# A hybrid RG-LRU and RWKV-7 block: the inverse's products in the second recurrence issued unit by unit, its values loaded two steps ahead, its outputs stored with half the transfers

## The chip, the core and the metric

One program runs on one core of a Trainium2 chip. The metric is the device time of one execution in microseconds (us); lower is better. The core has TensorE (PE; its weight loads are listed as PEld), VectorE (DVE), ScalarE (ACT), GpSimd (POOL), and SyncE (SP), whose queue issues all the transfers of this kernel. Matrix products leave TensorE into PSUM, and DVE or ACT copy them to SBUF.

## The reference, cut to what matters

The block takes 1024 latent tokens of width 1024 and 256 context tokens. Two token mixers run on the same normalised input: a gated linear recurrence (the first recurrence), and RWKV-7 (the second), of 16 heads, in two directions. Their outputs are gated, projected, summed into the stream, and followed by a SwiGLU layer and a final norm. The change lies in RWKV-7's scan over a state `S` of 64x64 for each head and direction, whose output of both directions is then summed, normalised per head and gated:

```
def wkv7_scan(r, w, k, v, a, b, S0):
    def step(S, inp):
        r_t, w_t, k_t, v_t, a_t, b_t = inp
        sa = jnp.einsum('dbhij,dbhj->dbhi', S, a_t)
        S = S * w_t[..., None, :] + sa[..., :, None] * b_t[..., None, :] + v_t[..., :, None] * k_t[..., None, :]
        y = jnp.einsum('dbhij,dbhj->dbhi', S, r_t)
        return S, y
...
ys, S = wkv7_scan(orient(two(rr)), orient(heads(decay)), orient(kd), orient(two(vv)),
                  orient(two(-kk)), orient(kk[None] * heads(a)), S0)
```

All is float32.

## The kernel before

The program has stages. `phase0_h`, `phase_ux` and `phase_a2` make the normalised input, its projections, the first recurrence (`lru_tiles`, in 11 tiles of 120 channels), and the operands of the second one. `phase_b` runs the second recurrence. `phase_c1` and `phase_c2` do the output projections and the SwiGLU layer. The framework schedules: it places each instruction in the in-order queue of its engine by priority (mostly the order of the program text) and by when it reckons the operands ready, so the end of `phase_a2` and the start of `phase_b` run together.

**The second recurrence in blocks.** The scan is taken 32 tokens at a time: 1280 tokens make `NSTEP` = 40 steps, steps 0 to 7 over the context, 8 to 39 over the latents (these give outputs). A unit is one head in one direction, 32 in all. `wkv_chain(k, a)` drives one half, 8 heads in both directions, so 16 units; the two halves `a` = 0 and 1 are generators that `phase_b` (L1134) advances in a fixed pattern, so that one half's products stand between a product and the copy it waits for in the other half. Within a half step, in this order:

- **ru**: 16 products of a unit's 128 rows by 32 columns, tile `skb` times `tvu`, into the first half of a PSUM tile `t` (`ru`). Four neighbours go to four column groups of TensorE. A copy then moves the result to `rs`.
- **X**: the inverse of a unit's 32x32 triangular system, times `rs`, into the second half of the same PSUM tile. The 32x32 inverses were made in `phase_a2` (`wkv_inverse`, on DVE), stored to DRAM (`x_d`, `xc_d`) and come back as `xc`, four steps a tile. Before the change a block-diagonal 128x128 matrix `xbd` is built from `xc` for each four units, by four DVE copies of 32 partitions a step (L1025, both halves at once; two buffers `xbd0`, `xbd1`, with zeros off the diagonal), and the half step needs 4 products of 128x128 (L1046). A switch `UT` in the text, off here, holds the other way: 16 products of 32x32 straight from `xc`.
- four copies of 32 partitions put the result into `tvu[96:128]`.
- **pn**: 16 products, the next state, into `pn`; two copies (at every second step a multiplication by the decay `pb`, L1063) move it to rows 0 to 63 of the next step's `tvu`.
- **py**: for latent steps 16 products give the output; a copy to `ys`, then four stores of 32 partitions to `y_d`, rows of 256 numbers each (L1013).

One f32 product shows as two matmuls in the trace. The copies of `wkv_chain` go to DVE and ACT in a fixed rota, two of five to DVE (L993).

**Values.** Rows 64 to 95 of `tvu` are the step's values, loaded from `v_d` by `new_tvu` one step ahead into one of two buffers for each half (L969).

**What runs beside it.** `lru_out` (PE group `pol`, L1107, with loads `lh`, `lu`, `olr`, `olg` and work on ACT, POOL and DVE) is a filler: 480 products of 128x128 by 512, dealt out after the products X of each half. `wkv_load` brings `ska`, `skb` and `xc` up to three steps ahead. From step 28 on `norms` runs `group_norm` for blocks of 128 tokens as both directions finish them; it loads `y_d` back in one transfer for each direction (L1246). The last two blocks follow in `phase_c1`.

**The queue of SP.** It is in order, and a transfer waits in it for its operands, for its buffer, and for an earlier transfer to land: the program gives each transfer one of eight semaphores in turn.

Of the kernel before, what the change touches and what calls it, by code (L numbers as in the profile page):

```python
# [16 lines left out]
P = 128  # L17
D = 1024
# [891 lines left out]
FPTS = ((0, 0), (38, 1), (40, 1))  # L910
UT = 0
NEND = 3
SETV = 0
SETDVE = 0
XDVE = 40
XACT = 0
PACE = 1
# [12 lines left out]
def wkv_setup(k):  # L930
# [4 lines left out]
    for i, t in enumerate(k.ska):  # L935
        nc.scalar.copy(t[0:64], bcast(k.ident[0:64, 0:64], 1, NU))
    if not UT:
        k.xbd = [z(f"xbd{i}", [P, 8, 4, 32]) for i in range(2)]
        for t in k.xbd:
            (nc.vector if SETDVE & 2 else nc.gpsimd).memset(t, 0.0)  # L940
    k.tvu = [[z(f"tvu{a}_{i}", [P, 2, 8, 64]) for i in range(2)] for a in range(2)]
    k.pb = z("pb", [P, 2, 20, KD])
# [22 lines left out]
def new_tvu(k, s, a):  # L965
    nc = k.nc
    src = pair(k.v_d.rearrange("(c s) f -> c s f", s=32), chunk_id(s, 0), chunk_id(s, 1))
    t = k.tvu[a][s % 2]
    nc.sync.dma_start(t[64:96].rearrange("p d h i -> p d (h i)"), src[:, :, a * 512:a * 512 + 512].rearrange("d s f -> s d f"))  # L969
    return t  # L970
# [14 lines left out]
def wkv_chain(k, a):  # L985
# [13 lines left out]
    def outputs(s, tvu):  # L999
        if s < 8:  # L1000
            return
        skb = k.skb[s % NRING]
        py = k.psb2.tile([P, 4, 64], F32, name=f"py{s}_{a}", tag="py", bufs=1)
        for v, g, gr, d, i in units:
            mm(py[gr, v], skb[:, unit(d, i), 0:32], tvu[:, d, i])
        ys = k.op.tile([P, 256], F32, name=f"ys{s}_{a}", tag="ys", bufs=4)
        copy(ys, py.rearrange("p v i -> p (v i)"))
        for d in range(2):
            r = 32 * chunk_id(s, d)
            for h in range(2):  # L1010
                g = 2 * d + h
                c = a * 512 + h * 256
                nc.sync.dma_start(k.y_d[d, r:r + 32, c:c + 256], ys[32 * g:32 * g + 32])  # L1013

    cur, nxt, prev = None, new_tvu(k, 0, a), None
    for t in k.tvu[a]:
        (nc.vector if a < SETV else nc.gpsimd).memset(t[96:P], 0.0)
    for s in range(NSTEP):
        ska, skb = k.ska[s % NRING], k.skb[s % NRING]
        if not UT:  # L1020
            xb = k.xbd[s % 2]
        if a == 0 and not UT:
            for g in range(4):
                gr = slice(32 * g, 32 * g + 32)
                (nc.scalar.copy if s < XACT else nc.vector.tensor_copy if s < XDVE else nc.gpsimd.tensor_copy)(xb[gr, :, g], k.xc[s // 4][gr, s % 4].rearrange("p a v t -> p (a v) t"))  # L1025
        prev, tvu = cur, nxt
        cur = tvu
        ahead = lambda: new_tvu(k, s + 1, a) if s + 1 < NSTEP else None
        if a == 1:
            nxt = ahead()  # L1030
        t = ps.tile([P, 2, 4, 64], F32, name=f"ru{s}_{a}", tag="ru", bufs=2)
# [6 lines left out]
        if a == 0:  # L1038
            if s > 0:
                outputs(s - 1, prev)  # L1040
            nxt = ahead()
            yield
        for v, g, gr, d, i in units if UT else ():
            mm(t[gr, 1, v], k.xc[s // 4][gr, s % 4, a, v], r[gr, v])
        for v in range(0 if UT else 4):
            mm(t[:, 1, v], xb[:, a * 4 + v].rearrange("p a b -> p (a b)"), r[:, v])  # L1046
        for g in range(4):
# [186 lines left out]
def group_norm(k, pool, ps, tb, out=None):  # L1234
# [9 lines left out]
    y1 = k.c1p.tile([P, NH, 64], F32, name="gy1_7") if tb == 7 else big("gy1")  # L1244
    for t, src in ((v, k.v_d), (g, k.gate_d), (y, k.y_d[0]), (y1, k.y_d[1])):
        nc.sync.dma_start(flat(t), src[tok])  # L1246
        for _ in range(GNY):
            yield
# [252 lines left out]
def scratch(k):  # L1501
# [15 lines left out]
    k.t1_d = t("t1_d", [D, SEQ])  # L1517
    k.y_d = t("y_d", [2, SEQ, D])

# [176 lines left out]
```

## Time and profile before

| | |
|---|---|
| median of 3 runs | 3172.0 us (3169.22 to 3175.68) |
| the profiled execution | 3170.86 us, of which the profile spans 3168.8 us |
| PE busy | 2772.7 us (87%), 20606 matmuls |
| DVE busy | 2010.8 us (63%) |
| ACT busy | 1410.4 us (45%) |
| POOL busy | 1037.3 us (33%) |

The profile is one execution. Busy time of PE is the union of its matmuls; a matmul's duration holds its way through the array, so neighbours overlap, and the pace of a group is read from the starts. "PEclk" is the granted share of TensorE's clock: 1.0 is 2.4 GHz, 0.5 is 1.2 GHz, a value between them a mixture over time. "Idle before" is an engine's idle time just ahead of a group, with what ended it.

### The profile page before, as it was taken

The numbers are of one execution on the slowest core, as the hardware profiler recorded it, in microseconds if no ns is written. First come the engines' busy times: TensorE is split into PE (matmuls) and PEld (weight loads), VectorE is DVE, ScalarE is ACT, GpSimd is POOL, SyncE is SP. The second block draws the span as 40 slices with busy tenths as digits, with TensorE's granted clock in tenths as the row PEclk, the third lists the DMA queues.
The fourth block names the chain that finished last, engine by engine and source line by source line (L and its number), as shares of the span: only waits on it lengthen the run. The fifth ranks groups of instructions, "written<-read, shape, count | busy, mean of one in ns | idle before, by whom it ended". The sixth has DMA issues, their size and how long they took to land. (4 is left out here: it accounts for less than half of the span.)

```text
span 3168.8 us, 53672 instructions
## 1 busy us (share of the span) xinstructions
PE 2772.7 (87%) x20606; PEld 2235.2 (71%) x20606; DVE 2010.8 (63%) x3067; ACT 1410.4 (45%) x2579; POOL 1037.3 (33%) x896
## 2 busy tenths in 40 slices
PE   5888888789898878887889878788899999999998
PEld 4767666667777666765666767566678888888888
DVE  7688989894667887878874434675686423232234
ACT  3465757474467555767333433344425111111114
POOL 4344435452445545666333220323441000000000
PEclk9999899999899878987558978788999999999999
DMA  5334333322455455555766777776772211111112
GB/s 201 105 107 128 115 109 118 111 76 74 142 145 143 114 123 128 131 140 136 192 189 213 220 210 206 222 240 220 266 284 85 98 57 54 37 57 40 46 57 71
DMA packets 374726, 428.96 MB, mean 135 GB/s; under 512 B 135446, under 2 KB 279238, under 8 KB 366534
## 3 DMA queue, kind: packets, MB, share of 16 engines
q1 hardware_dynamic: 374470, 425.53, 45.4%
q8 instruction: 163, 2.67, 0.4%
q14 instruction: 93, 0.76, 0.1%
HBM read 286.87 MB, written 126.26 MB: 130 GB/s over the span
## 5 line engine op out<-in xcount | busy, mean ns | idle before, releaser
L88 PE MATMUL pin<-h1024hi,whi 128*128 128x512 f32 (+1 forms) x1024 | 431.9, 422 | 47.0 <-DVE whi L230 15.2
L90 PE MATMUL pin<-h1024hi,wlo 128*128 128x512 f32 (+1 forms) x1024 | 425.8, 420 | 26.0 <-POOL wlo L231 16.8
L89 PE MATMUL pin<-h1024lo,whi 128*128 128x512 f32 (+1 forms) x1024 | 427.2, 417 | 4.1 <-DVE h1024lo L120 4.1
L231 POOL TENSOR_TENSOR wlo<-wraw,whi 128x512 fp32r<-128x512 f32 (+1 forms) x144 | 229.7, 1595 | 339.8 <-DVE whi L230 135.0
L88 PEld LDWEIGHTS pin<-h1024hi,whi 128*128 128x128 f32 (+1 forms) x1024 | 205.2, 201 | 100.8 <-DVE whi L230 21.3
L90 PEld LDWEIGHTS pin<-h1024hi,wlo 128*128 128x128 f32 (+1 forms) x1024 | 204.8, 200 | 80.6 <-POOL wlo L231 23.1
L89 PEld LDWEIGHTS pin<-h1024lo,whi 128*128 128x128 f32 (+1 forms) x1024 | 204.2, 199 | 51.3 <-DVE h1024lo L120 6.6
L54 ACT ACT_TABLE_LOAD x164 | 210.4, 1283 | 17.2 <-DVE gd L499 5.9
L990 PE MATMUL pn<-tvu,ska 128*64 128x64 f32 (+1 forms) x2496 | 159.8, 255 | 34.9 <-DVE tvu L993 20.1
L1444 DVE TENSOR_TENSOR sil<-sil,pfu 128x512 f32<-128x512 f32 x44 | 30.2, 687 | 243.2 <-PE pfu L90 243.2
L990 PEld LDWEIGHTS pn<-tvu,ska 128*64 128x64 f32 (+1 forms) x2496 | 122.8, 161 | 75.9 <-DVE tvu L993 23.3
L388 DVE SCALAR_TENSOR_TENSOR lxc<-lup,c_lru_conv_w,lxc 120x512 f32<-120x512 f32 (+3 forms) x198 | 159.4, 835 | 0.4
L1452 DVE SCALAR_TENSOR_TENSOR x<-pfo,modv,x 128x512 f32<-128x512 f32 (+1 forms) x112 | 74.2, 670 | 132.4 <-PE pfo L90 132.4
L990 PE MATMUL ru<-tvu,skb 128*32 128x64 f32 (+1 forms) x2560 | 107.7, 260 | 49.9 <-ACT tvu L993 26.0
L993 ACT COPY tvu<-ru 32x256 f32<-32x256 f32 x193 | 69.9, 362 | 151.8 <-DVE tvu L993 99.4
L68 ACT CAST whi_fi<-wraw_fi 128x1024 fp32r<-128x1024 f32 x48 | 50.6, 1053 | 168.3 <-PE pfg L89 53.0
L990 PE MATMUL ru<-rs,xbd 128*128 128x64 f32 x640 | 113.3, 335 | 12.4 <-ACT rs L993 8.3
L415 PE MATMUL pg<-lh,gw 120*120 120x512 f32 (+3 forms) x264 | 95.4, 373 | 32.4 <-DVE lh L398 29.7
L990 PEld LDWEIGHTS ru<-tvu,skb 128*32 128x32 f32 (+1 forms) x2560 | 69.5, 131 | 75.9 <-ACT tvu L993 28.5
L680 ACT COPY bc<-pm 32x256 f32<-32x256 f32 x160 | 98.5, 616 | 52.6 <-PE pm L676 50.3
L721 DVE TENSOR_TENSOR X<-X,it 128x62 f32<-128x62 f32 (+25 forms) x186 | 119.1, 640 | 3.9
L720 DVE TENSOR_TENSOR it<-bp,X 128x62 f32<-128x62 f32 (+25 forms) x186 | 118.3, 636 | 3.8
(374 smaller groups left out, 7660.8 us busy)
## 6 DMA issues: line engine op xcount, KB each, us to landing
skb<-skb_d SPq DMA_DIRECT2D x40, 1024.0 KB
wraw<-in_w_in_dram SPq DMA_DIRECT2D x142, 256.0 KB
wraw_fi<-in_w_ffn_in_dram SPq DMA_DIRECT2D x48, 512.0 KB
skb_d<-kr SPq DMA_DIRECT2D x160, 128.0 KB
ska_d<-km SPq DMA_DIRECT2D x160, 128.0 KB
skb_d<-km SPq DMA_DIRECT2D x160, 128.0 KB
ska<-ska_d SPq DMA_DIRECT2D x40, 512.0 KB
wmr<-in_w_modT_dram SPq DMA_DIRECT2D x32, 512.0 KB
```

The lines of the kernel that those rows point to most:

```text
L54: ins = self.nc.scalar.activation(*a, **b).ins
L88: nc.tensor.matmul(out, wh, xh, start=first, stop=False)
L89: nc.tensor.matmul(out, wh, xl, start=False, stop=False)
L90: nc.tensor.matmul(out, wl, xh, start=False, stop=last)
L231: (nc.gpsimd if INLO else nc.vector).tensor_tensor(lo, raw, hi.bitcast(F32), ALU.subtract)
L388: nc.vector.scalar_tensor_tensor(xc, tap(j), k.lcw[r, t, d, j:j + 1], xc, ALU.mult, ALU.add)
L415: nc.tensor.matmul(pg[r, g, 0:w], gw[r, v, g * LT:g * LT + rows(t)], m, start=(x == 0), stop=(x == len(passes) - 1))
L680: nc.scalar.copy(bc[g, :, 4 * i:4 * i + 4].rearrange("s t e h -> s h e t"), pm[64 * c + 32:64 * c + 64, :, d, :, 32:64])
L720: nc.vector.tensor_tensor(tv, bpt[:, :, t + 1:32, t:t + 1].to_broadcast(sh), X[:, :, t:t + 1, 0:t + 1].to_broadcast(sh), ALU.mult)
L721: nc.vector.tensor_tensor(X[:, :, t + 1:32, 0:t + 1], X[:, :, t + 1:32, 0:t + 1], tv, ALU.add)
L990: k.pe_last = nc.tensor.matmul(*a, **b, start=True, stop=True).ins.name
L1452: nc.vector.scalar_tensor_tensor(x, p[:, 0:n], k.modv[:, 40 + o, 0:1], x, ALU.mult, ALU.add)
```

## The change

The switch `UT` and its alternatives go; the branch that was off becomes the only one. Five things are different:

- X is 16 products of 32x32 for a half step, from `xc` and the unit's 32 rows of `rs`, each on its own 32 rows and 32 columns of TensorE. `xbd`, its clearing and its four copies a step are gone.
- `tvu` has three buffers for each half, and `new_tvu` is called for step `s + 2`.
- `y_d` is laid out in blocks of 32 tokens by 256 channels, and an output tile needs two stores of 64 partitions.
- `group_norm` therefore loads each direction of a block in four transfers, which are 32 partitions of four rows of 256.
- Line numbers fall by 8 to 20. The first recurrence has 11 tiles in both kernels; the diff does not touch it.

```diff
-    if not UT:
-        k.xbd = [z(f"xbd{i}", [P, 8, 4, 32]) for i in range(2)]
-        for t in k.xbd:
-            (nc.vector if SETDVE & 2 else nc.gpsimd).memset(t, 0.0)
-    k.tvu = [[z(f"tvu{a}_{i}", [P, 2, 8, 64]) for i in range(2)] for a in range(2)]
+    k.tvu = [[z(f"tvu{a}_{i}", [P, 2, 8, 64]) for i in range(3)] for a in range(2)]
...
-    t = k.tvu[a][s % 2]
+    t = k.tvu[a][s % 3]
...
         for d in range(2):
-            r = 32 * chunk_id(s, d)
-            for h in range(2):
-                g = 2 * d + h
-                c = a * 512 + h * 256
-                nc.sync.dma_start(k.y_d[d, r:r + 32, c:c + 256], ys[32 * g:32 * g + 32])
+            nc.sync.dma_start(k.y_d[d, chunk_id(s, d), 2 * a:2 * a + 2].rearrange("h t f -> (h t) f"), ys[64 * d:64 * d + 64])
 
-    cur, nxt, prev = None, new_tvu(k, 0, a), None
+    cur, nxt, nn, prev = None, new_tvu(k, 0, a), new_tvu(k, 1, a), None
...
-        if not UT:
-            xb = k.xbd[s % 2]
-        if a == 0 and not UT:
-            for g in range(4):
-                gr = slice(32 * g, 32 * g + 32)
-                (nc.scalar.copy if s < XACT else nc.vector.tensor_copy if s < XDVE else nc.gpsimd.tensor_copy)(xb[gr, :, g], k.xc[s // 4][gr, s % 4].rearrange("p a v t -> p (a v) t"))
...
-        ahead = lambda: new_tvu(k, s + 1, a) if s + 1 < NSTEP else None
+        cur, nxt = tvu, nn
+        ahead = lambda: new_tvu(k, s + 2, a) if s + 2 < NSTEP else None
...
-        for v, g, gr, d, i in units if UT else ():
+        for v, g, gr, d, i in units:
             mm(t[gr, 1, v], k.xc[s // 4][gr, s % 4, a, v], r[gr, v])
-        for v in range(0 if UT else 4):
-            mm(t[:, 1, v], xb[:, a * 4 + v].rearrange("p a b -> p (a b)"), r[:, v])
...
-    for t, src in ((v, k.v_d), (g, k.gate_d), (y, k.y_d[0]), (y1, k.y_d[1])):
-        nc.sync.dma_start(flat(t), src[tok])
+    for t, src in ((v, k.v_d), (g, k.gate_d), (y, 0), (y1, 1)):
+        if t is v or t is g:
+            nc.sync.dma_start(flat(t), src[tok])
+        else:
+            for c in range(4):
+                nc.sync.dma_start(flat(t)[32 * c:32 * c + 32].rearrange("t (b f) -> t b f", f=256),
+                                  k.y_d[src, 4 * tb + c].rearrange("b t f -> t b f"))
...
-    k.y_d = t("y_d", [2, SEQ, D])
+    k.y_d = t("y_d", [2, SEQ // 32, 4, 32, 256])
```

The scheduler works the whole order out anew. In the lists below `ru15_0` is ru (or, where it reads `rs15_0`, X) of step 15, half 0; `pol1_0` is the filler; the size is that of the product, and x16 stands for 16 alike in a row.

PE at latent step 15 before:

```order
L990 MATMUL ru15_0_17048<-rs15_0_17065,xbd1_14850 128x64 x4
L1107 MATMUL pol0_6_16574<-lhi0_9_15001,oll0_6_16566 128x512
L990 MATMUL pn14_1_17091<-tvu1_0_14855,ska2_14842 64x64
L990 MATMUL py14_1_17136<-tvu1_0_14855,skb2_14845 32x64 x2
L990 MATMUL pn14_1_17091<-tvu1_0_14855,ska2_14842 64x64 x15
L990 MATMUL py14_1_17136<-tvu1_0_14855,skb2_14845 32x64 x14
```

and after:

```order
L982 MATMUL ru15_0_17322<-rs15_0_17339,xc12_16554 32x64 x16
L1087 MATMUL pol0_6_16804<-lhi0_9_15009,oll0_6_16796 128x512
L982 MATMUL py14_1_17420<-tvu1_2_14854,skb2_14845 32x64 x16
L982 MATMUL ru15_1_17444<-tvu1_0_14852,skb0_14843 32x64 x16
L982 MATMUL pn15_0_17463<-tvu0_0_14849,ska0_14840 64x64
```

X is one unbroken run of 16 in place of one of 4.

PE at context step 3 before, beside operands of `phase_a2` (`pm`, `pkt`):

```order
L990 MATMUL pn3_0_15434<-tvu0_1_14854,ska0_14840 64x64
L676 MATMUL pm7_768_14624<-kr7_768_0_14585,kb7_768_0_14584 64x64 x13
L990 MATMUL pn3_0_15434<-tvu0_1_14854,ska0_14840 64x64 x4
L990 MATMUL ru3_1_15415<-rs3_1_15432,xbd1_14850 128x64 x4
L990 MATMUL pn3_0_15434<-tvu0_1_14854,ska0_14840 64x64 x11
```

and after:

```order
L982 MATMUL ru3_0_15400<-rs3_0_15417,xc0_14860 32x64 x16
L982 MATMUL ru3_1_15485<-tvu1_0_14852,skb0_14843 32x64 x16
L676 MATMUL pm7_512_14499<-kr7_512_0_14460,kb7_512_0_14459 64x64 x3
L982 MATMUL pn3_0_15504<-tvu0_0_14849,ska0_14840 64x64
L676 MATMUL pm7_512_14499<-kr7_512_0_14460,kb7_512_0_14459 64x64 x2
L692 MATMUL pbn7_512_14548<-c_rkblk_6145,kd07_512_0_14456 128x2 x2
L982 MATMUL pn3_0_15504<-tvu0_0_14849,ska0_14840 64x64 x8
L982 MATMUL ru3_1_15485<-rs3_1_15502,xc0_14860 32x64 x9
L982 MATMUL pn3_0_15504<-tvu0_0_14849,ska0_14840 64x64
L982 MATMUL ru3_1_15485<-rs3_1_15502,xc0_14860 32x64
```

Here X of half 1 and pn of half 0 go on alternating one by one, six times more after the last row. Counted over the order of PE as built, the recurrence's products form so many unbroken runs:

| | ru | X | pn | py | all |
|---|---|---|---|---|---|
| steps 0 to 7, before | 89 | 17 | 89 | 0 | 195 |
| steps 0 to 7, after | 89 | 72 | 123 | 0 | 284 |
| steps 8 to 39, before | 99 | 64 | 136 | 150 | 449 |
| steps 8 to 39, after | 93 | 72 | 116 | 165 | 446 |

The queue of SP around step 15 before, from the stores of one output tile to those of the second after it:

```order
L1013 DMA y_d_77<-ys15_0_17253 32x256 x4
L1094 DMA olr1_1_18259<-in_w_o_lru_dram 128x1280
L1083 DMA lh1_3_17633<-lru_d_61 128x512
L1083 DMA lh1_4_17643<-lru_d_61 128x512
L982 DMA ska0_14840<-ska0_d_70 64x2048
L982 DMA skb0_14843<-skb0_d_68 128x2048
L1013 DMA y_d_77<-ys15_1_17309 32x256 x4
L969 DMA tvu1_1_14856<-v_d_67 32x2x512
L969 DMA tvu0_0_14853<-v_d_67 32x2x512
L1013 DMA y_d_77<-ys16_0_17408 32x256 x4
```

and after:

```order
L1001 DMA y_d_77<-ys15_0_17543 64x256 x2
L974 DMA ska0_14840<-ska0_d_70 64x2048
L1063 DMA lh1_3_17965<-lru_d_61 128x512
L974 DMA skb0_14843<-skb0_d_68 128x2048
L1001 DMA y_d_77<-ys15_1_17609 64x256 x2
L961 DMA tvu1_0_14852<-v_d_67 32x2x512
L1063 DMA lh1_4_17975<-lru_d_61 128x512
L1064 DMA lu1_5_17986<-uy_d_62 128x512
L961 DMA tvu0_1_14850<-v_d_67 32x2x512
L1001 DMA y_d_77<-ys16_0_17714 64x256 x2
```

Over this piece the queue holds 19 transfers before and 13 after, three of each the filler's. The load of half 0's values just ahead of the stores of `ys16_0` is for step 18 before and for step 19 after.

## Rows read from the trace of the kernel before

**Rows 1.** The profile's page: busy us, share, instructions of each engine.

```profile
PE 2772.7 (87%) x20606; PEld 2235.2 (71%) x20606; DVE 2010.8 (63%) x3067; ACT 1410.4 (45%) x2579; POOL 1037.3 (33%) x896
```

**Rows 2.** Busy time of each engine by stretch (columns in the header).

```profile
core 0: us, PE busy (x) PEld busy (x) DVE busy (x) ACT busy (x) POOL busy (x), PEclk, DMA share, GB/s
1490.00:1706.00 216.00, 174.92 (x1636) 131.99 (x1634) 165.82 (x296) 80.60 (x165) 75.09 (x75) 0.58 0.72 202
1706.00:2200.00 494.00, 406.48 (x7013) 326.38 (x7006) 250.38 (x433) 191.26 (x455) 134.18 (x74) 0.83 0.72 213
```

**Rows 3.** Groups, 1706 to 2200: xcount | busy us, mean ns | idle before.

```profile
L990 PE MATMUL ru<-rs,xbd 128*128 128x64 f32 x512 | 86.4, 323 | 10.0 <-ACT rs L993 5.8 <-DVE rs L993 3.8 <-issue 0.3
L990 PE MATMUL ru<-tvu,skb 128*32 128x64 f32 x2024 | 64.0, 249 | 37.1 <-ACT tvu L993 21.8 <-DVE tvu L1063 8.8 <-DMA tvu<-v_d 5.4
L1025 DVE COPY xbd<-xc 32x256 f32<-32x256 f32 x120 | 52.4, 437 | 31.1 <-PE ru L990 28.2
```

**Rows 4.** The same columns, 1490 to 1706.

```profile
L990 PE MATMUL ru<-rs,xbd 128*128 128x64 f32 x128 | 26.9, 381 | 2.4 <-ACT rs L993 2.4
L1025 DVE COPY xbd<-xc 32x256 f32<-32x256 f32 x40 | 14.6, 364 | 2.1 <-PE ru L990 1.6
```

**Rows 5.** Timeline of PE, upper clock: start us, us, what, count.

```profile
1705.44 0.65 PE L990 MATMUL ru<-tvu,skb 128*32 128x64 f32 x32
1706.03 1.15 PE L990 MATMUL pn<-tvu,ska 128*64 128x64 f32 x32
1707.11 1.10 PE L990 MATMUL ru<-rs,xbd 128*128 128x64 f32 x8
1708.14 0.31 PE L990 MATMUL ru<-tvu,skb 128*32 128x64 f32 x4
...
1709.26 0.33 PE L990 MATMUL pn<-tvu,ska 128*64 128x64 f32 x2
1709.52 0.30 PE L990 MATMUL py<-tvu,skb 128*32 128x64 f32 x2
1709.75 0.68 PE L990 MATMUL pn<-tvu,ska 128*64 128x64 f32 x16
```

**Rows 6.** Timeline of PE at the lower clock.

```profile
1681.24 0.42 PE L990 MATMUL ru<-tvu,skb 128*32 128x64 f32 x2
1681.59 0.48 PE L990 MATMUL pn<-tvu,ska 128*64 128x64 f32 x2
...
1688.84 0.44 PE L990 MATMUL ru<-tvu,skb 128*32 128x64 f32 x8
...
1690.72 1.97 PE L990 MATMUL ru<-rs,xbd 128*128 128x64 f32 x8
1692.62 1.07 PE L990 MATMUL ru<-tvu,skb 128*32 128x64 f32 x28
1693.62 0.80 PE L1107 MATMUL pol<-llo,olh 128*128 128x512 f32 x1
```

**Rows 7.** Waits, 1706 to 2200, for whom: us, times, longest.

```profile
DVE xbd L1025 <- PE ru L990: 28.2, 13, 7.5
ACT lu L54 <- DMA lu<-uy_d: 13.2, 6, 5.1
```

**Rows 8.** Waits in SP's queue, 1706 to 2200, same columns.

```profile
SPq L1013 <- DMA skb<-skb_d: 54.0, 19, 4.1
SPq L1246 <- DMA y_d<-ys: 7.8, 3, 3.9
```

**Rows 9.** Output stores: issue time in SP's queue, ns min/median/max.

```profile
L1013 SPq DMA_DIRECT2D y_d<-ys x256: 302/419/2002, 1715.2 to 2196.5; - x128
```

**Rows 10.** Timeline of SP where the recurrence ends.

```profile
2192.72 4.07 SPq L1013 DMA_DIRECT2D y_d<-ys  x8
2198.06 0.33 SPq L1246 DMA_DIRECT2D gy<-y_d  x1
```

More of the change, by code (lines that the diff above doesn't have):

```diff
@@ L910 @@
 FPTS = ((0, 0), (38, 1), (40, 1))
-UT = 0
 NEND = 3
 SETV = 0
-SETDVE = 0
-XDVE = 40
-XACT = 0
 PACE = 1
@@ L1019, in wkv_chain @@
         ska, skb = k.ska[s % NRING], k.skb[s % NRING]
-        if not UT:
-            xb = k.xbd[s % 2]
-        if a == 0 and not UT:
-            for g in range(4):
-                gr = slice(32 * g, 32 * g + 32)
-                (nc.scalar.copy if s < XACT else nc.vector.tensor_copy if s < XDVE else nc.gpsimd.tensor_copy)(xb[gr, :, g], k.xc[s // 4][gr, s % 4].rearrange("p a v t -> p (a v) t"))
         prev, tvu = cur, nxt
-        cur = tvu
-        ahead = lambda: new_tvu(k, s + 1, a) if s + 1 < NSTEP else None
+        cur, nxt = tvu, nn
+        ahead = lambda: new_tvu(k, s + 2, a) if s + 2 < NSTEP else None
         if a == 1:
-            nxt = ahead()
+            nn = ahead()
         t = ps.tile([P, 2, 4, 64], F32, name=f"ru{s}_{a}", tag="ru", bufs=2)
@@ L1040, in wkv_chain @@
                 outputs(s - 1, prev)
-            nxt = ahead()
+            nn = ahead()
             yield
-        for v, g, gr, d, i in units if UT else ():
+        for v, g, gr, d, i in units:
             mm(t[gr, 1, v], k.xc[s // 4][gr, s % 4, a, v], r[gr, v])
-        for v in range(0 if UT else 4):
-            mm(t[:, 1, v], xb[:, a * 4 + v].rearrange("p a b -> p (a b)"), r[:, v])
         for g in range(4):
```

## The prediction

> **What bounds the kernel now.** I read the page first: TensorE is busy 87% of the span [rows 1], so a gain must either shorten its work or close its gaps. The table by stretch says where the second recurrence stands: its context steps run from about 1490 to 1706 us beside the end of the operands, its latent steps from 1706 to 2200 [rows 2]. In the first stretch PE is busy 174.9 of 216 us at a granted clock of 0.58, and DVE, which makes the inverses there, is busy 165.8; neither alone sets the end. In the second PE is busy 406.5 of 494 us, 82%, at 0.83; DVE and ACT stand at half or less. So the latent stretch is bounded by PE's own work, by 87.5 us of gaps between products, and by the clock: 0.58 means that 16% of the stretch ran at 2.4 GHz and the rest at 1.2, 0.83 means 66%. The groups show that X is a large part of the work, 86.4 us busy for 64 half steps [rows 3] and 26.9 us for 16 [rows 4], and the timeline shows its pace from start to start: 1.03 us at the upper clock, where ru, also 16 products, takes 0.59 [rows 5]; at the lower clock 1.90 us, where 28 of ru's 32 matmuls take 1.00, so all take 1.14 [rows 6].
>
> **The change, part by part.** The sum is made against the profiled execution, 3170.86 us, 1.1 under the median of the three runs.
>
> X unit by unit, latent steps. The trace has no product of 32x32. Its nearest row is ru: the same count, the same 64 columns streamed, four neighbours on four column groups. I take ru's pace. That saves 0.44 us for a half step at the upper clock and 0.76 at the lower; with 66% and 34% that is 0.55, and over 64 half steps 35 us. One cost: X and the filler before had one shape, now they differ, and a change of shape is not free. Its price can be read where single products alternate: 20 pieces of ru and pn take 7.60 us at the lower clock, 0.38 each, where two matmuls in a run take 0.07 (ru) to 0.13 (pn), so 0.28 extra; at the upper clock pieces of two take 0.26 and 0.23, so some 0.19 extra [rows 5, 6]. X now meets the filler once in each of 64 half steps; at up to 0.22 that is 0 to 14 us, and I take 7. Otherwise the latent steps have as many runs as before (446 for 449 in the order). That leaves 28 us of PE's work. A shorter group gains only where something queued follows at once; I count PE's busy share, 82%: **23 us**. Ends: 35, and a loss of 90 if products of different rows don't overlap (the second rival).
>
> X unit by unit, context steps. Here the order has 284 runs for 195, mostly X and pn in turn. The gain of 16 half steps at 16% and 84% is 16 x 0.71 = 11 us; 89 more pieces at 0.27 cost 24. The net 13 us is PE's, in a stretch where PE has 41 us of gaps and the steps also wait for the inverse; I take half, **a loss of 6** (ends: a loss of 13, a gain of 11).
>
> The copies to `xbd`. In the latent stretch 120 go, 52.4 us of DVE, and with them 28.2 us in which DVE's queue stood before such a copy until X had freed its buffer [rows 3, 7]; DVE's copies of the recurrence were queued behind it. DVE is not the bound; of its time I count PE's idle share, 18%: 9 us (0 to 14). In the first stretch 40 go, 14.6 us [rows 4], from an engine busy 77% with the inverse on it; I take half, 7 (0 to 15). Together **16 us**. The clearing of `xbd` and of the third value buffers are a few GpSimd instructions ahead of the recurrence.
>
> Values two steps ahead. PE's waits before ru that ended with this load are 5.4 us [rows 3]; the load now has a step more to land: **5 us**. Its own wait in SP's queue stays, since the buffer is freed by the same products; what is queued behind it is `ska`, `skb` and the filler's loads, as before.
>
> Half the stores. 128 issues of 0.42 us (median) go [rows 9], 54 us of SP's queue. They also were the ones that stood for an earlier transfer: 54.0 us of waits of a store for `skb` to land [rows 8], since a semaphore comes round after eight transfers; with 13 in place of 19 in the piece shown, the eighth after `skb` comes later. Against that the blocks' loads of `y_d` go from 2 to 8 for each of 8 blocks, 48 more issues, 20 us, each of which waits in the queue for its stores to land (up to 3.9 us [rows 8]), with `ska`, `skb` and values behind it. Little of the queue's time reaches PE: the filler's late loads hold ACT for 13.2 us [rows 7], and a fifth of that is 3. I take **3 us**; ends: a loss of 10, a gain of 15.
>
> At the end of the recurrence 8 stores in a row take 4.07 us and then the last blocks' loads follow [rows 10]: four stores fewer, 1.7 us, against six issues more, 2.5. **A loss of 1.**
>
> Sum: -23 + 6 - 16 - 5 - 3 + 1 = -40, so 3131 in the profiled execution and **3132** against the median.
>
> **The rivals.** *The clock gives more.* PE's work costs about 1.9 times as much at the lower clock (1.90 to 1.03, 1.14 to 0.59). If smaller gaps take the lower share of the latent stretch from 34% to 25%, 406 x (1.225 / 1.306 - 1) = -25 us more, 3107; halved, -48, 3084. For it: fewer instructions on DVE and SP in front of the copies that PE waits for. Against: in the first stretch a busy share of 81% went with 0.58 [rows 2]. Chance 0.18.
>
> *Products on different rows don't overlap* (slower). ru's neighbours differ in columns and share their rows; those of X differ in both, and no row shows neighbours on different rows that write into one PSUM tile. If such products go one at a time, the pace follows from the rows: with four column groups a matmul starts every 18 ns (0.59 / 32), with two (pn, 1.08 / 32) every 34, so with one every 68. X then takes 2.2 us for 1.03 at the upper clock and some 4.1 for 1.90 at the lower: 64 x 1.5 + 16 x 2.0 = 128 us more, with the shape changes 159; with a fifth of it in PE's gaps and the other gains of 24 kept, about 3275. It turns into a loss as soon as X's matmuls come every 33 ns or more at the upper clock. For it speaks only that nothing shows the contrary. Against it: ru's four neighbours already write into one PSUM tile at once, and X's outputs lie on the same four partition groups. The Trainium skill speaks for this rival: its page "TensorEngine Tiling (Array Packing)", section "Gotcha 1: PSUM Pressure", says that row tiles must write to different PSUM banks, since two of them cannot use one bank at the same time. By that page X would take its second price here and the sum would be a loss of about 100 us; no run here shows it yet. Chance 0.10.
>
> *The broken runs eat it.* The context steps lose all 24 us of the price and set the end there (no gain from DVE either): +13. The latent steps gain half of theirs, -12, and half of DVE's, -5, since ACT and DVE are late next. With 3 for the values: about 3165. For it: PE waited for ACT and DVE in 31 us of the ru row alone [rows 3], and no copy of the chain gets shorter. Chance 0.15.
>
> **How the numbers follow.** Forecast (3112 to 3158) 0.55, the clock 0.18, broken runs 0.15, no overlap 0.10, and 0.02 for a queue blocked by the new loads. A measurement of this kernel can tell about 0.2%, 6 us, from no change. Faster by more: 0.55 + 0.18 and a third of the broken runs, 0.78; slower by more: 0.10 + 0.02 = 0.12; within: 0.10. The range for 8 in 10 runs from 3092, leaving out the stronger half of the clock's case, to 3176, leaving out the slower cases.
>
> **What would show it.** X as 32 matmuls in 0.6 to 0.7 us at the upper clock: the main term holds; 2 us: the second rival. DVE's busy time in the recurrence down by 65 us, the wait of stores for `skb` gone from SP's list, no PE gap ended by `v_d`. The context steps no shorter than before, or longer by up to 10 us, with X and pn alternating. The granted clock of the latent stretch still 0.8 to 0.87; over 0.9 and the first rival holds. The prediction is wrong if the latent steps don't fall below 470 us for 494, or if the stages before 1490 us or after the recurrence change by more than a few us.

## The result and the profile after

The changed kernel takes 3139.5 us (median of 4 runs, 3131.11 to 3148.93), the kernel before 3170.6 on the same chips: a ratio of 0.9895, 95% interval 0.987 to 0.992, so 1.05% faster, 33 us (the two medians lie 31 us apart). The forecast was 3132. The total is close by luck: the runs below show that three of its terms were wrong, by 13 to 23 us each, and cancelled each other.

The profiled execution of the changed kernel spans 3136.6 us. I take the recurrence from its first product ru to its last py, cut where step 8 begins (the copy after its first ru). The first view is the time by stretch, columns as in [rows 2], once for all work and once for the filler's tile `pol` alone:

```profile
1504.30:1700.30 196.00, 169.50 (x1930) 118.08 (x1930) 130.26 (x238) 64.74 (x136) 56.71 (x60) 0.58 0.67 181
1700.30:2157.80 457.50, 364.14 (x8560) 275.12 (x8560) 189.08 (x309) 197.29 (x464) 135.10 (x78) 0.90 0.82 238
```

```profile
1504.30:1700.30 196.00, 16.62 (x44) 9.48 (x44) 0.00 (x0) 0.58 0.67 181
1700.30:2157.80 457.50, 128.35 (x392) 76.38 (x392) 9.59 (x14) 0.90 0.82 238
```

The same cut of the kernel before, filler alone (PE, PEld, DVE; then clock, DMA share, GB/s):

```profile
1502.10:1706.20 204.10, 31.09 (x90) 20.71 (x90) 1.38 (x2) 0.58 0.71 199
1706.20:2193.90 487.70, 119.60 (x346) 71.74 (x346) 8.30 (x12) 0.83 0.72 213
```

So the recurrence starts 2 us later, its context steps take 196 us for 204, its latent steps 457.5 for 487.7, and what follows takes 4 us more (3136.6 - 2157.8 = 978.8, for 974.9): -32 in all. The two lengths must be read with the filler: 46 of its products moved from the context steps into the latent ones. The context steps lost 14.5 us of filler (31.09 to 16.62) and became only 8 shorter; the latent steps took in 8.8 us more and still became 30 shorter.

In the latent steps PE idles about as long as before (457.5 - 364.1 = 93.4 us; 87.5 by [rows 2]), and the clock rose from 0.83 to 0.90: 20% of the stretch at 1.2 GHz for 34%. The groups of that stretch (xcount | busy us, mean ns | idle before):

```profile
L982 PE MATMUL ru<-tvu,skb 128*32 128x64 f32 x2016 | 52.8, 230 | 18.0 <-issue 11.6 <-DVE tvu L985 2.8 <-ACT tvu L985 2.1
L982 PE MATMUL ru<-rs,xc 32*32 32x64 f32 x2048 | 51.7, 236 | 22.1 <-issue 13.5 <-ACT rs L985 4.6 <-DVE rs L985 4.0
```

X took 86.4 us before [rows 3]. ru, whose products are the same, fell from 64 to 52.8, and its idle time from 37.1 to 18.0. The clock is part of that: 29% of ru's matmuls ran at 1.2 GHz before and 10% after, which by their pace at either level before is worth some 5 us (an estimate); for the rest no run gives a reason. But a releaser is new: "issue", PE waiting for nothing that the profile shows. The timeline (start us, us) gives X's pace at the upper clock (first pair) and the lower (second pair):

```profile
1855.24 0.65 PE L982 MATMUL ru<-rs,xc 32*32 32x64 f32 x32
1855.82 0.50 PE L1087 MATMUL pol<-llo,olh 128*128 128x512 f32 x1
...
2153.78 1.07 PE L982 MATMUL ru<-rs,xc 32*32 32x64 f32 x32 [0.25 <-ACT rs L985]
2154.79 0.80 PE L1087 MATMUL pol<-lhi,oll 128*128 128x512 f32 x1
```

From start to start X takes 0.58 us and 1.01 us, for 1.03 and 1.90 before [rows 5, 6]. The context steps show the price of broken runs at the lower clock:

```profile
1601.58 0.47 PE L982 MATMUL pn<-tvu,ska 128*64 128x64 f32 x2
1601.98 0.42 PE L982 MATMUL ru<-rs,xc 32*32 32x64 f32 x2
1602.33 0.48 PE L982 MATMUL pn<-tvu,ska 128*64 128x64 f32 x2
1602.73 0.42 PE L982 MATMUL ru<-rs,xc 32*32 32x64 f32 x2
```

Two matmuls every 0.38 us; X's busy time in that stretch rose from 26.9 us [rows 4] to 36.0 (one group again, from 1490 to 1700 us):

```profile
L982 PE MATMUL ru<-rs,xc 32*32 32x64 f32 x512 | 36.0, 289 | 7.0 <-ACT rs L985 6.9
```

Waits in SP's queue, 1700 to 2160 us (us, times, longest), against [rows 8]:

```profile
SPq L1230 <- DMA y_d<-ys: 31.8, 10, 5.2
...
SPq L1001 <- DMA skb<-skb_d: 11.2, 6, 4.2
```

The stores' wait for `skb` fell from 54.0 us to 11.2; the new loads of `y_d` wait four times as long as the old.

### The profile page after: what moved, and what is told of

Same layout as the page of the kernel before. It is cut to its first block, busy times and chain, and to the rows that moved or that the text cites. A ratio compares the mean times of both kernels' runs of the same rounds, so it can differ in the third digit from the quotient of the medians.

```text
span 3136.6 us, 57219 instructions
## 1 busy us (share of the span) xinstructions
PE 2740.9 (87%) x22526; PEld 2183.7 (70%) x22526; DVE 1924.8 (61%) x2907; ACT 1410.3 (45%) x2579; POOL 1032.1 (33%) x896
## 5 line engine op out<-in xcount | busy, mean ns | idle before, releaser
L90 PE MATMUL pin<-h1024hi,wlo 128*128 128x512 f32 (+1 forms) x1024 | 426.7, 421 | 24.8 <-POOL wlo L231 15.7
L982 PE MATMUL ru<-tvu,skb 128*32 128x64 f32 (+1 forms) x2560 | 97.0, 245 | 25.1 <-issue 11.6
L230 DVE CAST whi<-wraw 128x512 fp32r<-128x512 f32 (+1 forms) x144 | 76.7, 533 | 68.7 <-PE pin L89 41.0
L430 POOL TENSOR_TENSOR lg<-lg,lxc 120x512 f32<-120x512 f32 (+3 forms) x66 | 93.7, 1433 | 63.3 <-ACT lg L54 59.8
```

The costliest lines, as they stand in the source:

```text
L90: nc.tensor.matmul(out, wl, xh, start=False, stop=last)
L430: nc.gpsimd.tensor_tensor(gi, gi, xc, ALU.mult)
L982: k.pe_last = nc.tensor.matmul(*a, **b, start=True, stop=True).ins.name
```

## What holds PE with no releaser: its code

The new "issue" waits are seen in mid-run. PE's timeline of the kernel after:

```profile
1823.72 0.52 PE L982 MATMUL ru<-rs,xc 32*32 32x64 f32 x20
1827.85 0.41 PE L982 MATMUL ru<-rs,xc 32*32 32x64 f32 x12 [3.60 <-issue]
```

Twenty of X's 32 matmuls run, then PE stands 3.6 us, though all 32 need the same two tiles. In that gap one packet of the instruction queue passes, between 1825.4 and 1826.5 us (DMA view; packets, MB, share):

```profile
q8 instruction: 1, 0.02, 5.0%
```

The two pages say whose queue that is, the kernel before first, the kernel after second, with PE's row of the kernel after:

```profile
q8 instruction: 163, 2.67, 0.4%
```

```profile
q8 instruction: 178, 2.92, 0.4%
PE 2740.9 (87%) x22526; PEld 2183.7 (70%) x22526; DVE 1924.8 (61%) x2907; ACT 1410.3 (45%) x2579; POOL 1032.1 (33%) x896
```

PE has 1920 more matmuls and as many weight loads than in [rows 1]; 0.25 MB more for 3840 instructions is 65 bytes each, and 15 more packets are one for each 256. (The Trainium skill, "Perfetto Trace Analysis", section "The 4-stage abstract model", gives 64 bytes for an instruction; the trace agrees.) Counting PE's gaps of 0.7 us and over with no releaser from 1500 us to the end of the recurrence: 1 of 1.3 us before, 12 of 29.2 us after, and each of the 12 ends 1.2 to 1.7 us after a 16 KB packet has passed. Such a packet passes only once in 8 us there (83 of them), so that this isn't chance. (The expectations below leave out one wait in each kernel: 11 and 26 us for the 12 here, 15 and 26 us for the 16 of after_one_ahead.) ru, X and py take about 15 ns a matmul at the upper clock; 128 of them, one packet's worth, are done in 2 us. The experiments below take this as a theory.

## The experiments

The first theory is the prediction's sum: X with its copies -33 us, early loads -5, stores -3 + 1. The second is that code waits take back some of X's gain and that other parts carry more. Ratios are to the kernel before on the same chip, with 95% intervals; 0.1% is 3.2 us. The lengths are cut as above; "pieces" are the unbroken runs of the recurrence's products in steps 0 to 7, in PE's order as built. Starts and lengths come from one execution each, and the executions of one kernel lie 5 to 23 us apart, so that single lengths are good to several us only. What follows the recurrence is not in the table: it takes 971 to 979 us, but 988 in stores_alone, 989 in after_four_stores and 999 in stores_four_new_layout; no run was made for that.

| kernel | ratio | interval | first ru at, us | steps 0-7, us (pieces; filler) | steps 8-39, us (clock; filler) |
|---|---|---|---|---|---|
| before | 1 | | 1502.1 | 204 (195; 90) | 488 (0.83; 346) |
| after | 0.9895 | 0.987 to 0.992 | 1504.3 | 196 (284; 44) | 458 (0.90; 392) |
| x_alone | 0.9883 | 0.9858 to 0.9907 | 1477.8 | 174 (209; 6) | 509 (0.87; 430) |
| x_copies_kept | 0.9973 | 0.9958 to 0.9987 | 1497.9 | 197 (279; 54) | 486 (0.87; 382) |
| x_alone_pad | 0.9951 | 0.9934 to 0.9969 | 1498.3 | 208 (273; 48) | 471 (0.86; 388) |
| stores_alone | 0.9924 | 0.9905 to 0.9942 | 1507.7 | 207 (195; 90) | 447 (0.88; 346) |
| stores_four_new_layout | 1.0040 | 1.0026 to 1.0055 | 1499.1 | 208 (195; 90) | 477 (0.85; 346) |
| after_four_stores | 0.9981 | 0.9968 to 0.9994 | 1504.8 | 196 (284; 44) | 481 (0.88; 392) |
| after_one_ahead | 0.9821 | 0.9801 to 0.9842 | 1486.7 | 170 (209; 6) | 489 (0.88; 430) |
| after_one_ahead_pad | 0.9870 | 0.9847 to 0.9894 | 1498.7 | 209 (273; 48) | 446 (0.89; 388) |
| one_ahead_pad_2kb | 0.9859 | 0.9840 to 0.9879 | 1497.4 | 208 (273; 48) | 444 (0.89; 388) |
| one_store | 0.9818 | 0.9799 to 0.9837 | 1479.6 | 170 (209; 6) | 480 (0.87; 430) |
| more_code | 1.0240 | 1.0218 to 1.0262 | 1485.7 | 240 (426; 6) | 548 (0.82; 430) |
| filler_four | 1.0011 | 0.9998 to 1.0025 | 1482.8 | 199 (304; 6) | 516 (0.84; 433) |

### X alone, its copies, and the memory

x_alone:

```diff
-UT = 0
+UT = 1
```

> Only the switch UT is set to 1 in the kernel before: X is 16 products of 32x32 for a half step, xbd and its four copies a step are gone; two value buffers, loads one step ahead, four stores a half step stay. By the prediction's terms this part is -23 (latent X) + 6 (context X) - 16 (copies) = -33 us against the kernel before, ratio about 0.990. A second theory, from the trace of the changed kernel: X's own gain is larger, about 42 us over all steps, the code that PE has to load for 1920 more products takes some 25 us of it back as waits of PE that nothing releases (11 waits before PE's products of 1 us and over, 26 us, against 1 of 1.3 us before), and less time at the lower clock (91 us of the latent steps for 167) gives some 30 us. If X brings both, these waits number 8 or more here and the granted clock of the latent stretch is 0.88 or more; if the clock came from the stores or the early loads, it stays at 0.83 to 0.85 and the kernel gains 15 us or less.

It gained 1.17%, 37 us: by the total, the prediction's -33 holds. Much of the clock came with it (0.87, just under the 0.88 that the second theory asked for), and "issue" ended 15.7 us of waits before X and ru.

x_copies_kept, on top of it:

```diff
-    if not UT:
+    if 1:
         k.xbd = [z(f"xbd{i}", [P, 8, 4, 32]) for i in range(2)]
...
-        if a == 0 and not UT:
+        if a == 0:
```

> As x_alone, but DVE still makes the four copies into xbd in every step, which nothing reads. It prices the copies: the prediction's term for them is 16 us, so -17 us against the kernel before. If the pace of X and the clock carry the gain and DVE's time is off the path, it is within 5 us of x_alone. If the gain of the change is DVE's time, it is within 5 us of the kernel before.

The copies seemed to be worth 0.9%, 28 us, more than the prediction's 16 and most of the gain. But the two kernels differ in a second thing: x_alone has no `xbd`, 8 KB a partition, and its recurrence begins 20 us earlier. x_alone_pad takes the copies away and keeps the memory:

```diff
+    k.pad = z("pad", [P, 2048])
     k.tvu = [[z(f"tvu{a}_{i}", [P, 2, 8, 64]) for i in range(2)] for a in range(2)]
```

> x_alone with a tile of 8 KB a partition, never written or read, in the recurrence's pool where xbd stood; no copies. x_copies_kept was 24.5 us slower than x_alone. If that is DVE's time for the copies, the pad costs nothing and this kernel stays within 5 us of x_alone (3138 us). If it is the memory (without xbd's 8 KB the pool no longer reaches buffers that the stage before it frees late, and the recurrence starts at 1478 us in place of 1498 to 1504), this kernel is 15 to 25 us slower than x_alone, near x_copies_kept (3163 us), its first product ru comes at about 1500 us, and the copies themselves cost what is left to x_copies_kept.

The tile that nothing touches costs 0.68%, 22 us. What is left to DVE's copies is 0.22% (7 us; with both intervals, 0 to 14). In x_copies_kept they stand in DVE's queue as they did before: 25.9 us for `xc` to land, where it was 28.2 for X. The first products ru (start times from first to last) of x_alone, and of x_alone_pad:

```profile
L990 PE MATMUL ru<-tvu,skb x76: 283/311/314, 1477.8 to 1499.4; 64*32 64x64 f32 x64, 128*32 128x64 f32 x12
```

```profile
L991 PE MATMUL ru<-tvu,skb x48: 282/308/311, 1498.3 to 1499.5; 64*32 64x64 f32 x48
```

and their context steps by stretch, columns as in [rows 2], again x_alone first:

```profile
1477.80:1651.50 173.70, 140.43 (x2070) 103.95 (x2074) 125.41 (x234) 69.55 (x152) 47.13 (x57) 0.64 0.74 194
```

```profile
1498.30:1706.60 208.30, 169.38 (x1934) 118.14 (x1936) 134.21 (x239) 67.75 (x140) 59.79 (x61) 0.58 0.67 181
```

With the pad the first load of values stands 16 places later in SP's queue and is issued at 1486.1 us for 1466.6; ACT's first writes to `ska` come at 1484.2 for 1468.0 and wait for a transfer of `phase_a2` (`gr_d`, 1.1 us), which they don't in x_alone. That fits a pool of the recurrence that now reaches over buffers of `phase_a2` that come free late; the traces don't show addresses. The steps that follow are also more broken (273 pieces for 209) and run at 0.58 for 0.64, though x_copies_kept, with 279 pieces, ran at 0.64 too. So X's own gain at equal memory, copies included, is 0.49%, 15.5 us, half of what the prediction gave these terms; without the copies' part it is the 0.27%, 9 us, of x_copies_kept (4 to 13).

### The third value buffers

after_one_ahead undoes this part of the change:

```diff
-    k.tvu = [[z(f"tvu{a}_{i}", [P, 2, 8, 64]) for i in range(3)] for a in range(2)]
+    k.tvu = [[z(f"tvu{a}_{i}", [P, 2, 8, 64]) for i in range(2)] for a in range(2)]
...
-    t = k.tvu[a][s % 3]
+    t = k.tvu[a][s % 2]
...
-        ahead = lambda: new_tvu(k, s + 2, a) if s + 2 < NSTEP else None
+        ahead = lambda: new_tvu(k, s + 1, a) if s + 1 < NSTEP else None
```

> The changed kernel with two value buffers and loads one step ahead, as before the change; X unit by unit and two stores a half step stay. By the prediction 5 us slower than the changed kernel (-35 us against the kernel before), with waits of PE before ru that end with the values' load back, some 5 us. If the waits for code are what now sets the pace, the earlier loads bring nothing and the time is that of the changed kernel within 3 us.

Neither expectation held: it is 0.74% faster than the changed kernel, 23 us. The third buffers take just the 8 KB that `xbd` gave up. after_one_ahead_pad puts the 8 KB back as a pad, after_one_ahead being otherwise as it was:

> after_one_ahead (X unit by unit, two stores, two value buffers) with the same unused tile of 8 KB, which is what the third value buffers take. after_one_ahead was 3119 us, the changed kernel 3139. If the memory makes that difference, this kernel is at 3138 to 3146 us with its first product ru at 1500 to 1505 us, and what it lies above the changed kernel is what the loads two steps ahead bring at equal memory (the prediction's 5 us). If the loads two steps ahead themselves cost the 20 us, it stays near 3119 us.

15.5 of the 23 us are the memory. What remains, 0.25% (and 0.30% between x_alone_pad and after_four_stores, the same pair with four stores), is what early loads cost at equal memory, 8 to 10 us. The intervals of both pairs overlap, the second's barely: that early loads do not gain the 5 us is clear, that they lose is likely. They did what they were for: waits of PE for `v_d` were 9.2 us in x_alone_pad and 3.2 in after_four_stores, 4.2 in after_one_ahead_pad and none in the changed kernel. Where the loss lies is not one place in the traces (first ru 6 us later, context steps 12 shorter, latent steps 10 to 12 longer, what follows 5 and 18 longer), and it stays open.

one_ahead_pad_2kb has 512 in place of 2048 in the pad:

> after_one_ahead with an unused tile of 2 KB a partition in place of the 8 KB of after_one_ahead_pad. If the memory acts as a boundary (the pool just reaches a buffer that is freed late), 2 KB cost as much as 8: the first product ru at about 1498 us, ratio 0.987 as with 8 KB. If it acts by amount, a quarter of the 0.5% is lost: ratio 0.983, start within 4 us of 1487.

2 KB cost 0.38%, 8 KB 0.49%, and both start at 1497 to 1499 us, with the first load of values at the same late place: it is a boundary, and after_one_ahead lies less than 2 KB under it.

### The stores

stores_alone puts the new layout, two stores and eight loads into the kernel before, as in the diff of the change.

> The kernel before with the new layout of y_d, two stores a half step and four loads for each direction of a block; X by xbd, copies, loads one step ahead as before. The prediction's terms: -3 + 1, so 2 us faster than the kernel before. From the pairs on the chip with X unit by unit (x_alone to after_one_ahead, -20; after_four_stores to the changed kernel, -25) a gain of 20 us or more, if the stores act by themselves; if they act only where PE is faster, under 8 us.

A gain of 0.76%, 24 us, by themselves; 0.6 to 0.9% in every other pair (x_alone to after_one_ahead, x_alone_pad to after_one_ahead_pad, after_four_stores to after). The last pair:

> The changed kernel with the old layout of y_d, four stores a half step and one load for each direction of a block; X unit by unit and values two steps ahead stay. By the prediction 2 us slower than the changed kernel (3 for the stores, less 1 at the end), with stores in SP's queue that wait for skb some 40 us again. If the queue's time reaches PE more than by a fifth, 8 us slower or more; if the 48 more loads of y_d cost more than the stores, faster than the changed kernel by some us.

It is 27 us slower than the changed kernel. stores_four_new_layout asks whether layout or number does it:

```diff
-        for d in range(2):
-            nc.sync.dma_start(k.y_d[d, chunk_id(s, d), 2 * a:2 * a + 2].rearrange("h t f -> (h t) f"), ys[64 * d:64 * d + 64])
+        for g in range(4):
+            nc.sync.dma_start(k.y_d[g // 2, chunk_id(s, g // 2), 2 * a + g % 2], ys[32 * g:32 * g + 32])
```

> stores_alone, but each output tile goes in four stores of 32 partitions again, each into a block of 32 KB of the new layout: the number of stores of before, the layout and the eight loads a block of after. stores_alone gained 24 us on the kernel before (3149 for 3170 us) where the prediction had 2. If the number of transfers in SP's queue did that (128 issues of 0.4 us and their waits for earlier transfers), this kernel is at or above the kernel before, ratio 0.998 to 1.004, and its stores wait for skb some 40 us again. If the layout did it (contiguous blocks in place of rows 4 KB apart), it stays near 0.992.

The layout gains nothing; with the loads added it loses 0.4%. By its trace the loss falls after the recurrence (999 us for 975), while its latent steps are 11 us shorter than before. SP's waits, PE's ru row and a row of ACT's waits show what two stores change. stores_alone (SP's waits, 1706 to 2150 us; PE's group and ACT's waits in the latent steps):

```profile
SPq L1009 <- DMA skb<-skb_d: 13.9, 6, 3.3
```

```profile
L990 PE MATMUL ru<-tvu,skb 128*32 128x64 f32 x2016 | 61.0, 235 | 22.9 <-ACT tvu L993 12.7 <-DMA tvu<-v_d 4.3 <-DVE tvu L1059 3.4
ACT olg L54 <- DMA olg<-gl_d: 22.4, 5, 7.6
```

stores_four_new_layout, the same rows:

```profile
SPq L1009 <- DMA skb<-skb_d: 51.9, 19, 4.2
```

```profile
L990 PE MATMUL ru<-tvu,skb 128*32 128x64 f32 x2016 | 63.1, 247 | 48.3 <-ACT tvu L993 29.1 <-DMA tvu<-v_d 13.4 <-DVE tvu L1059 2.5
ACT olg L54 <- DMA olg<-gl_d: 40.8, 8, 8.7
```

With four stores in a row the eighth transfer after `skb` is a store of outputs for 21 of the 29 loads of `skb` in the latent steps, and SP stands until 1 MB has landed; with two stores it is one for 9 of 29, and most of that wait goes. The loads of values and of the filler stand behind it: PE waits 13.4 us for values with four stores and 4.3 with two, ACT 71 and 49 us for the filler's loads (`olg`, `olr` and `lu` together), and PE 29.1 and 12.7 us for ACT's copies ahead of ru. That ACT's waits are what makes these copies late is read from the rows, not tested by itself. PE's idle time ahead of ru halves, and the clock rises: at the same number of matmuls (6974 and 6978) the latent steps of stores_alone are

```profile
1715.10:2162.20 447.10, 380.01 (x6974) 305.67 (x6974) 237.23 (x423) 183.79 (x435) 120.34 (x70) 0.88 0.78 228
```

against, in the kernel before,

```profile
1706.20:2193.90 487.70, 400.18 (x6978) 321.22 (x6976) 247.53 (x430) 191.26 (x455) 129.53 (x72) 0.83 0.72 213
```

That is 20 us less idle and 20 less busy at a higher clock. (Some 13 us of it go again after the recurrence, 988 us for 975.)

one_store goes on in that direction, on top of after_one_ahead. `y_d` is laid out by step, and one store takes all 128 partitions:

```diff
-            mm(py[gr, v], skb[:, unit(d, i), 0:32], tvu[:, d, i])
+            mm(py[32 * (2 * (g % 2) + d):][:32, v], skb[:, unit(d, i), 0:32], tvu[:, d, i])
...
-        for d in range(2):
-            nc.sync.dma_start(k.y_d[d, chunk_id(s, d), 2 * a:2 * a + 2].rearrange("h t f -> (h t) f"), ys[64 * d:64 * d + 64])
+        nc.sync.dma_start(k.y_d[s - 8, 2 * a:2 * a + 2].rearrange("b d t f -> (b d t) f"), ys)
```

> after_one_ahead with y_d laid out by step, so that an output tile of 128 partitions goes in one store; the rows of py are put in the order head pair, direction; four loads for each direction of a block stay. 64 issues fewer in SP's queue. If each issue saved in front of the queue is worth what the first 128 were (24 us, with 48 loads added), 64 are worth 8 to 14 us and this kernel comes to about 3108 us, ratio 0.979. If it was the waits of stores for skb that counted (54 us before the change, 11 after), there is little left, and it is within 4 us of after_one_ahead (ratio 0.982).

64 issues fewer bring nothing that can be measured. That speaks against the queue's issue time and for whom it stood waiting for, but it doesn't part the two: the stores' waits for `skb` that were left in after_one_ahead, 16.5 us in the latent steps, went as well (0.2), and the loads of `y_d` waited longer. Those loads, after_one_ahead first, one_store second:

```profile
SPq L1230 <- DMA y_d<-ys: 30.6, 9, 4.9
```

```profile
SPq L1230 <- DMA y_d<-ys: 42.6, 10, 8.7
```

So it is shown that two stores for four bring the gain; that they bring it by the wait for `skb` fits the rows, and no run changes that wait alone.

one_store and after_one_ahead are the two fastest kernels here, 0.7 to 0.8% under the changed one.

### The code

more_code, on top of after_one_ahead:

```diff
+        for v, g, gr, d, i in units:
+            mm(t[gr, 1, v, 0:4], k.xc[s // 4][gr, s % 4, a, v], r[gr, v, 0:4])
         for v, g, gr, d, i in units:
             mm(t[gr, 1, v], k.xc[s // 4][gr, s % 4, a, v], r[gr, v])
```

> after_one_ahead with a second set of X's 16 products in each half step, ahead of the real ones, of the first 4 columns only; the real ones write over them. 2560 more matmuls and as many weight loads. PE's own work for them is some 32 x 8 to 10 ns, 0.3 us a half step, 20 to 25 us in all 80. If PE's waits that nothing releases (26 us in after_one_ahead) are waits for code, they grow to 45 us or more, with 20 more 16 KB packets in the code queue, and the kernel takes 35 to 60 us more (3155 to 3180 us). If they are something else, they stay at 20 to 30 us and the kernel takes 15 to 25 us more.

The packets are 20 more, as expected (198), and the waits of PE with no releaser in the latent steps rise from 27 us to 48. PE's rows (us, times, longest), after_one_ahead, 1656 to 2146 us:

```profile
PE ru L982 <- issue: 20.8, 13, 3.6
...
PE pn L982 <- issue: 4.4, 3, 2.3
...
PE py L982 <- issue: 1.9, 3, 1.4
```

and more_code, 1725 to 2273 us:

```profile
PE ru L982 <- issue: 29.6, 15, 3.6
...
PE py L982 <- issue: 8.8, 4, 3.0
PE pn L982 <- issue: 7.7, 4, 2.7
...
PE pol L1089 <- issue: 2.4, 2, 2.1
```

The time rose by 4.2%, 133 us, more than twice what I allowed. The added matmuls start 12 ns apart on the mean, 30 us in all. Most of the 133 is neither that nor code: the context steps broke into 426 pieces and took 70 us more at 0.52, and the latent steps ran at 0.82. As a price of code this kernel is no measure; as a sign that these waits are code it is.

filler_four:

```diff
-FILLAT = (3, 7)
+FILLAT = (1, 3, 5, 7)
```

> after_one_ahead with the filler's products dealt out at four places of a step in place of two (also after each half's ru or py). Its trace has 15 waits of PE of 0.7 us and over that nothing releases, 26 us, each ended some 1.4 us after a 16 KB packet of the code queue. If they come from runs of short products that use up code faster than it is loaded (ru, X and py take 15 ns a product), shorter runs between filler products make them fewer than 10, under 15 us; the price is up to 64 more changes of shape at 0.15 to 0.25 us, some 10 us. So within 10 us of after_one_ahead (3119 us), to either side. If the waits don't depend on the order, they stay at 20 us or more.

The gaps of 0.7 us and over fell from 16 (29 us) to 7 (12 us), as the theory of code said, and the kernel lost 1.9%, 60 us, against it: context steps in 304 pieces for 209, and the clock of the latent steps at 0.84. Shorter runs save code waits and cost far more elsewhere.

## Why the prediction came out right

**X in the latent steps (-23).** The size of the step was right where it was read from rows: 0.58 and 1.01 us against the 0.59 and 1.14 taken from ru, 86.4 to 51.7 us busy, the forecast's gross 35. The rival in which products on different rows take turns is refuted by the same rows. A row of the kernel before already spoke against it, and the prediction says that there is none: in `phase_a2` neighbours of `pm` lie on two row groups and two column groups and write into one PSUM tile, though the two row groups into different halves of 2 KB a partition. At the upper clock 32 of them take 0.62 us:

```profile
1000.81 0.69 PE L676 MATMUL pm<-kr,kb 64*64 64x64 f32 x32
1001.43 0.61 PE L692 MATMUL pbn<-c_rkblk,kd 128*128 128x2 f32 x4
```

The Trainium skill's page "TensorEngine Tiling (Array Packing)", section "Gotcha 1: PSUM Pressure", says that row tiles cannot use one PSUM bank at a time; here the 16 products of X, on four row groups, write into one PSUM tile of 2 KB a partition in 0.58 us, and the measurement decides. What failed is the step from PE's work to time, where 82% of the work saved was counted and no rival or term had code in it: code waits are 12 to 33 us in every kernel with X unit by unit, more_code aside (1 to 3 us in those that use `xbd`). In x_copies_kept PE's busy time in the latent steps is 25 us less than before and its idle time 24 us more; 15 of the 24 are waits with no releaser.

**X in the context steps (+6).** The mechanism holds: pieces of two in 0.38 us, X's row +9 us. The size is not settled: the stretch became 8 us shorter with 14.5 us less filler in it, so 6 longer if all of the filler's time counts, where with 7 for the copies I had it 1 shorter. The many pieces come with the memory: with X unit by unit, 273 to 284 in every kernel that holds `xbd`, third buffers or a pad, 209 in x_alone, after_one_ahead and one_store.

**The copies (-16).** Off in size: 7 us at equal memory, 0 to 14. DVE's time counted for less than the shares taken (18% and a half). But taking `xbd` away had a second effect that I passed over: its 8 KB were worth 16 to 22 us more. The change spent them again at once on the third value buffers.

**Values two steps ahead (-5).** Wrong, and likely in sign: the waits of PE for `v_d` went, as the term said, and the kernel lost 8 to 10 us all the same, at equal memory. The step that failed is counting a wait that PE no longer has as time won.

**Half the stores (-3).** The largest error: -20 to -27 in the four pairs. "Little of the queue's time reaches PE" was the wrong step, whichever part of that time it was. I priced the loads that ACT waits for by a fifth of 13.2 us, which is one row of three; the others, 1706 to 2200 us, are

```profile
ACT olg L54 <- DMA olg<-gl_d: 26.8, 6, 6.6
ACT olh L68 <- DMA olr<-in_w_o_lru_dram: 17.5, 3, 9.4
```

And I left out that the 54.0 us of [rows 8] stood ahead of every load in the queue, those of values among them. The row was on the table, and so was the rule of eight; only its price was guessed low, and the bound of 15 was passed. The reading that the eighth transfer after `skb` comes later doesn't follow from the piece shown, where it is the second store of `ys16_0` in both kernels; over all latent steps it is a store of outputs 21 times in 29 before and 12 in 29 after.

**The end (+1).** 4 us longer after the recurrence: a few, as allowed.

By the measured terms: -15.5 for X with its copies, -25 for the stores, +8 for the early loads, and nothing for the memory, which was freed and taken again: -32.5, where -33 was measured. This sum must come out, since x_alone_pad and after_one_ahead_pad are steps on one way from the kernel before to the changed one; that the terms hold by themselves rests on the other pairs (the stores 20 to 27 us, the early loads 8 and 10). Against them the forecast had -33, -2 and -5: errors of 17, 23 and 13 us that leave 7. The right total was luck in that.

The clock rose as far as the first rival said: 0.90, at its line, with 20% of the latent steps at 1.2 GHz, between its two cases. The time it promised for that, 3084 to 3107, did not come; a gain of the clock stands in the measured terms and was in none of the forecast's. It rose in stores_alone (0.88) and x_alone_pad (0.86) alike, so it belongs to neither part alone.

Of what was to be seen: X's pace, no PE gap ended by `v_d`, the latent steps under 470 us, the stages around them within a few us, all came; DVE lost 82 us for 65 (154 + 248 to 130 + 189); the stores' wait for `skb` shrank to 11.2 and did not vanish. The context steps were to be no shorter than before and were, by the filler that left them; the clock was to stay at 0.8 to 0.87 and did not.

## What to carry to other kernels

When a queue's list of waits shows a transfer standing for another one's landing, price it by all that stands behind it, and try first whether fewer or other transfers in a row move that wait elsewhere; here a second halving of the stores, with little of that wait left, brought nothing more. A change that frees or takes on-chip memory can have a second effect where pools of two stages share it: keep an unused tile of the same size beside the experiment before any term is believed. When a product is split into many small ones, count PE's instructions too, and look for gaps in mid-run that nothing releases.

## What the runs showed of the hardware

PE's code comes in packets of 16 KB, one for each 256 instructions, over the DMA engines that the data use; such a packet took 0.9 to 2 us here. Runs of matmuls at 15 ns use one up in 2 us, and PE then stood up to 4.0 us at a time, 12 to 33 us in a recurrence of 650 to 715 (more_code aside). I had not expected that a product's cost could lie in how many instructions it has.

Neighbours on different rows and columns of TensorE that write into one PSUM tile of 2 KB a partition keep the pace of neighbours on different columns alone (0.58 and 0.59 us for 32).

The granted clock fell in short pieces, each after a stretch in which PE had stood for part of the time (0.5 to 5 us). With idle time much the same (87.5 and 93.4 us of the latent steps) it fell as often, 20 and 19 times, but for less long, 8 us before and 5 after on the mean, so that the share at 1.2 GHz was 34% before and 20% after. Why, the runs don't tell.
